# A hybrid layer on one core: norm_g held in PSUM, the Newton step in scalar form, one instruction for the key low parts, tile 5's counts on DVE, and a schedule from other durations

## The chip, the core and the metric

The kernel runs on one core of one Trainium2 chip. The core has a matrix engine (TensorE, PE in the profile; its weight loads are PEld), three engines for the element-wise work (VectorE or DVE, ScalarE or ACT, GpSimd or POOL) and SyncE (SP), which here issues every DMA. They share SBUF (128 partitions) and PSUM (8 banks of 128 x 2 KB), in which PE puts its products. The metric is the time of one execution on the device in microseconds (us); lower is better.

## What is computed

One layer with 1024 tokens of 1024 channels, in float32. The input projection of the normed x feeds a pooling mixer (A), an attention over keys that an indexer picks (B, "dsa") and an attention with forget gates (C, "fox"); each is gated, and an output projection, the residual and a last norm follow. Cut to what matters:

```python
h = rmsnorm(x, norm_g)                       # y * rsqrt(mean(x*x) + 1e-6) * g
(pv, pg, dq, dk, dv, dg, iq, ik, iw, fq, fk, fv, fg, ff) = split_columns(h @ w_in)
a_out = pool_mixer(pv, pool_w, pool_scale) * silu(pg)   # windows 2, 4, 8, 16
# B: the indexer scores every key, 8 heads of 32 channels, and keeps the 256 best a query
score = sum_h(iw[h] * relu(iq[h] . ik))      # only keys of the query's 64-chunk or before
b_out = softmax_attention(dq, dk, dv, keys=top_k(score, 256)) * silu(dg)
# C: F = cumsum(log_sigmoid(ff + fox_bf)); causal
c_out = softmax_attention(fq, fk, fv, bias=F[t] - F[s]) * silu(fg)
out = rmsnorm(x + concat(a_out, b_out, c_out) @ w_out, final_g)
```

## The kernel before

**Order.** The kernel doesn't run in the order in which it is written. Each instruction is given to `Plan.op` with its engine, what it reads and writes, a duration and a priority; `schedule` then goes through all of them once, on a model clock, and always takes the instruction that can start first on its engine (of those that can start together, the one of lowest priority number). The durations come from `t_act`, `t_dve`, `t_pool` and `t_mm`, by the number of columns (a negative number marks a transpose on PE). The result is one fixed list per engine, and a buffer for every result: SBUF and PSUM are cut into tags, each with a few slots, which are handed out in the same walk. Priorities put the norms first (`PR_NORM` 0), then the indexer's scores (`PR_DOT` 1), weights (1.5), the attention (`PR_AT` 2), the search (`PR_SEL` 5) and the projections (`PR_PJ` 10); the evictions of projections, `PR_EV`, have -10. The projections are so the work that PE does while it has nothing more urgent.

**Numbers in two parts.** For most products a float32 value is split into a high part in the fast format and a low part, the difference. A product is then three (high x high, high x low, low x high), all through line L462. So behind most transposes and weight loads stand two instructions: ScalarE copies the high part, DVE or POOL subtracts the low part.

**Stages.** Tiles are 128 tokens.

1. Norms and indexer projection, for tiles 0 to 7. `norm`: ScalarE sums the squares; `rstd` makes mean + eps (L481, L484) on DVE, the power -0.5 on POOL (L486) and one Newton step on DVE in three instructions of one column (L487, L489, L490); DVE multiplies x by that and by norm_g (L515, two halves); PE transposes (L522); ScalarE copies the high part (L526) and DVE subtracts the low part (L527). The norm weights are brought to 128 partitions by two PE products with ones, which ScalarE copies to SBUF (L418). `idx_proj` makes 302 columns a tile (L462): ScalarE copies 288 of them (L544), DVE takes the six of the forget gate (L545) and the eight head weights (L547). `idx_k` repeats the key four times (POOL, `rep`, L553), transposes it (L563), and has ScalarE copy it (L565) and DVE turn the rows 32 to 63 and 96 to 127 into low parts (L567, two instructions of 32 partitions).
2. Scores, `idx_tile`, for tiles 2 to 7: PE products per head (L595), ScalarE's relu (L599), DVE's multiply and add (L603, L607).
3. Search for the 256th best score of each query, `search`: 31 iterations over the bits of the threshold. In each one the scores of the tiles 2 to 7 are counted against the present threshold, those of `on_act` (5, 6, 7) by ScalarE (L771, 768 to 1024 columns), those of 2, 3, 4 by DVE (L776, 384 to 640 columns); then DVE decides in three instructions of six columns (L790, L792, L793). `finish` (L805 to L849) makes the masks on DVE; for the tiles of `on_act` it has a few more instructions. PE does the projections in this stretch: fox k and q, values, gates, and the pooling mixer's input.
4. `gate`: ScalarE's tanh into a buffer of tag `th` (L736), DVE's multiply with the product (L738), which ends the use of the PSUM bank; then it is stored. The tag `th` has two buffers. `pool_tile` uses the same tag: window sums on POOL, DVE's L1073, a product by PE (L1081), DVE's multiply with the stored gate in a `th` buffer (L1085) and the store of that to `mix`.
5. Attention, six units each of fox and dsa: products (L919, L922), DVE with bias or mask (L930), exponential (L941), transposes (L956), high and low parts (L963, L965), products with the values (L969, L974).
6. Output projection, eight tiles.

All DMAs go through SP's one queue (L365), also in the list's order. PSUM banks are shared by tags: `pj` (projections) has three, `s` (scores; also the key transposes and the pool products) has 2 and 3, `pn` (transposes of the norm) has 4, 5 and 7. PE begins with 60 products on the identity matrix that nothing reads (L408).

## Time and profile before

| what | value |
|---|---|
| time, median of 3 runs | 649.95 us (649.72 to 651.6) |
| the profiled execution's own time | 651.98 us |
| its span (first to last instruction) | 650.2 us |
| PE busy in it | 627.8 us, 97% |
| DVE, ACT, POOL busy | 474.4, 425.5, 201.6 us |

The span is what the profile's rows lie in, and all positions are counted from its start. "Busy" of PE counts a product as long as it is in the engine at the rate it has, not at its best. In the table of stretches the granted clock is given as a share: 1.00 is the 2.4 GHz level, 0.50 the 1.2 GHz one. A timeline names what an instruction waited for in brackets, the idle time of its engine ahead of it and the instruction that ended it.

### The profile page before, as it was taken

What the parts mean: (1) busy time and instruction counts of PE and PEld (TensorE: products, weight loads), DVE (VectorE), ACT (ScalarE), POOL (GpSimd) and SP (SyncE); (2) the same over time, 40 slices, a digit from 0 to 9 for tenths busy, and PEclk for the clock granted to TensorE, in tenths of its full rate; (3) what the DMA queues carried; (4) which work ended last, traced back from release to release, by engine and by line L of the source; (5) the groups of instructions that cost most, each with busy time, mean ns of one, the idle gap of its engine ahead of it and who ended that gap; (6) DMA issues with size and microseconds to landing.
All of it is one profiled execution on the core that took longest, in us unless ns stands there. A gap on an engine that the chain in (4) does not pass through costs nothing. (4 is left out here: it accounts for less than half of the span.)

```text
span 650.2 us, 10279 instructions
## 1 busy us (share of the span) xinstructions
PE 627.8 (97%) x3280; PEld 529.0 (81%) x3280; DVE 474.4 (73%) x1187; ACT 425.5 (65%) x945; POOL 201.6 (31%) x218
## 2 busy tenths in 40 slices
PE   8799999999999999799999999999999999999995
PEld 7698777789988999588888888888888687788884
DVE  5987999877776887889997768766757877643322
ACT  6645678698899888513478776688477879622121
POOL 3510212450017640126252614312131625232211
PEclk9999999999999999989999999999999999999999
DMA  8616453461026337845669678599946554547311
GB/s 241 192 53 176 148 156 109 129 184 44 0 87 157 103 127 208 196 124 138 176 200 247 202 211 212 155 252 270 242 162 169 166 165 148 157 161 226 120 43 66
DMA packets 95380, 102.72 MB, mean 158 GB/s; under 512 B 8055, under 2 KB 64471, under 8 KB 95326
## 3 DMA queue, kind: packets, MB, share of 16 engines
q1 hardware_dynamic: 95326, 102.07, 55.3%
q8 instruction: 26, 0.43, 0.3%
q14 instruction: 28, 0.23, 0.1%
HBM read 72.09 MB, written 29.96 MB: 157 GB/s over the span
## 5 line engine op out<-in xcount | busy, mean ns | idle before, releaser
L462 PE MATMUL bank<-RA 128*128 128x512 f32 (+2 forms) x2016 | 481.4, 378 | 3.8 <-DVE FA L738 3.8
L462 PEld LDWEIGHTS bank<-RA 128*128 128x128 f32 x2016 | 359.7, 189 | 54.0 <-DVE FA L738 4.3
L771 ACT ACTIVATE FA<-FA 128x768 bf16<-128x768 f32 (+2 forms) x96 | 99.6, 1037 | 15.8 <-DVE FA L793 12.4
L695 POOL TENSOR_TENSOR RA<-FA,RA 128x512 fp32r<-128x512 f32 x44 | 60.2, 1382 | 145.7 <-ACT RA L694 129.4
L941 ACT ACTIVATE FA<-FA 128x512 f32<-128x512 f32 (+3 forms) x144 | 86.8, 605 | 19.2 <-DVE FA L936 19.0
L963 ACT ACTIVATE RA<-bank 128x512 fp32r<-128x512 f32 (+1 forms) x120 | 64.5, 552 | 41.5 <-PE bank L956 36.7
L930 DVE CUSTOM_DVE_ANT_0 FA<-bank,FA 128x512 f32<-128x512 f32 (+3 forms) x144 | 77.3, 550 | 19.6 <-PE bank L922 11.2
L965 DVE TENSOR_TENSOR RA<-bank,RA 128x512 fp32r<-128x512 f32 (+1 forms) x120 | 74.1, 634 | 20.2 <-ACT RA L963 18.5
L956 PE MATMUL bank<-FA 128*128 128x128 f32 x432 | 72.6, 275 | 1.0 <-ACT FA L941 1.0
L776 DVE TENSOR_SCALAR_CACHE_REDUCE FA<-FA 128x384 bf16<-128x384 f32 (+2 forms) x96 | 71.2, 742 | 1.9
L956 PEld LDWEIGHTS bank<-FA 128*128 128x128 f32 x432 | 53.6, 140 | 20.9 <-ACT FA L941 4.3
L607 DVE SCALAR_TENSOR_TENSOR FA<-FA 128x512 f32<-128x512 f32 (+3 forms) x70 | 52.8, 776 | 2.3
L919 PE MATMUL bank<-RA 128*128 128x512 f32 (+3 forms) x144 | 52.1, 362 | 0.3 <-DVE FA L930 0.2
L974 PE MATMUL bank<-RA 128*128 128x512 f32 (+3 forms) x144 | 50.1, 376 | 0.5 <-DVE RA L965 0.5
L922 PE MATMUL bank<-RA 128*128 128x512 f32 (+3 forms) x144 | 50.1, 352 | 0.0
L599 ACT ACTIVATE FA<-bank 128x512 f32<-128x512 f32 (+3 forms) x80 | 39.7, 527 | 15.1 <-PE bank L595 6.2
L926 POOL TENSOR_TENSOR FA<-FA 128x128 f32<-128x128 f32 x48 | 29.1, 610 | 65.4 <-DVE FA L930 45.5
L969 PE MATMUL bank<-RA 128*128 128x512 f32 (+3 forms) x144 | 45.4, 341 | 0.3 <-DVE FA L1003 0.3
L1123 POOL TENSOR_TENSOR RA<-FA,RA 128x1024 fp32r<-128x1024 f32 x8 | 19.2, 2399 | 46.4 <-ACT RA L1122 35.3
L1135 DVE TENSOR_TENSOR FA<-bank,FA 128x512 f32<-128x512 f32 x16 | 11.0, 687 | 30.9 <-PE bank L462 30.9
L1007 POOL TENSOR_TENSOR FA<-FA 128x512 f32<-128x512 f32 x12 | 16.1, 1348 | 56.0 <-DVE FA L1003 35.9
L919 PEld LDWEIGHTS bank<-RA 128*128 128x128 f32 x144 | 27.1, 188 | 6.2 <-DVE FA L930 2.5
(145 smaller groups left out, 689.1 us busy)
## 6 DMA issues: line engine op xcount, KB each, us to landing
FA<-in_w_in_dram SPq DMA_DIRECT2D x60, 256.0 KB, 3.8
FA<-in_x_dram SPq DMA_DIRECT2D x15, 512.0 KB, 4.1
RA<-qk_fq SPq DMA_DIRECT2D x12, 512.0 KB, 8.2
RA<-qk_dq SPq DMA_DIRECT2D x12, 512.0 KB, 11.2
RA<-qk_dk SPq DMA_DIRECT2D x18, 256.0 KB, 6.0
...
```

Source lines behind the costliest of these rows:

```text
L462: M(lambda: nc.tensor.matmul(p()[:, :n], fa(), fb(), start=st, stop=sp), n, keys, [p], pr)
L607: V(lambda rl=rl, w=w, acc=acc, wc=wc: nc.vector.scalar_tensor_tensor(acc(), rl()[:, :w], wc(), acc(), op0=OP.mult, op1=OP.add), w, [rl, ( ...
L695: G(lambda raw=raw, s=s: nc.gpsimd.tensor_tensor(Wl()[:, s, :], raw(), f32(Wh()[:, s, :]), op=OP.subtract), 512, [raw, (Wh, kh)], [(Wl, kh ...
L771: A(lambda c=c, i=i, jk=jk, s=s: nc.scalar.activation(jk(), SC[i](), AF.Sign, bias=s(), scale=-1.0, accum_out=cn()[:, c:c + 1]), n, sck(i) ...
L776: V(lambda c=c, i=i, jk=jk, s=s: nc.vector.tensor_scalar(jk(), SC[i](), s(), None, op0=OP.is_lt, op1=OP.add, accum_out=cn()[:, c:c + 1]), ...
L919: M(lambda s=s, k=k, n=n, j=j, hd=hd: nc.tensor.matmul(s()[:, :n], q()[:, hd, j * 128:j * 128 + 128], k()[:, hd, :n], start=True, stop=False),
L922: M(lambda s=s, k=k, n=n, j=j, hd=hd: nc.tensor.matmul(s()[:, :n], q()[:, 2 + hd, j * 128:j * 128 + 128], k()[:, hd, :n], start=False, sto ...
L930: V(lambda s=s, Pt=Pt, n=n, u=u, j=j, mx=mx, bias=bias: nc.vector.tensor_tensor_reduce(Pt()[:, :n], s()[:, :n], bias()[:, u * 512:u * 512 ...
L941: A(lambda Pt=Ps[j][u], n=n, j=j, u=u, hd=hd, nm=nm: nc.scalar.activation(Pt()[:, :n], Pt()[:, :n], AF.Exp, bias=nm()[:, j:j + 1], accum_o ...
L956: M(lambda pt=pt, j=j, d=d, Pt=Ps[j][kb // 4], c=kb % 4 * 128: nc.tensor.transpose(pt()[:, j * 128 - d:j * 128 - d + 128], Pt()[:, c:c + 1 ...
L963: A(lambda ph=ph, pt=pt, c=c: nc.scalar.activation(ph()[:, c], pt()[:, c], AF.Copy), n, [pt], [ph], pr, psum=True)
L965: V(lambda ph=ph, pl=pl, pt=pt, c=c: nc.vector.tensor_tensor(pl()[:, c], pt()[:, c], f32(ph()[:, c]), op=OP.subtract), n, [pt, ph], [pl], pr)
```

## The change

In the programs' text, ahead of the plan:

- `norm_g` stays in PSUM. The two products with ones go to a new tag `gb` in the banks 2 and 3 (those of tag `s`), ScalarE's two copies L418 are gone, and DVE's norm multiply reads its factor from there. The key transposes move from tag `s` to `pn`.
- The Newton step, before (v * r0) * r0, then times -0.5 plus 1.5, then times r0, is written as three `tensor_scalar` with the power r0 as a scalar operand. The first, v * -0.5, doesn't need r0. It stands in the output norms too.
- The two L567 become one instruction on 128 partitions, with a column of 0 and -1 that tells which rows become low parts.
- L545 and L547 go to POOL and read ScalarE's copy, which now takes all the columns to 302, at a priority 0.5 later.
- Tile 5's counts go from ScalarE to DVE: per iteration DVE counts four tiles, ScalarE two.

And what the plan believes:

- A lock: an instruction of DVE with two inputs in SBUF (`two`) or of a fast form (`fast`), and one of POOL over 4 columns, can't run at the same time in the plan.
- Durations: ScalarE with a sum 0.1 us longer, a search count another 0.02; PE products 0.01 us longer, transposes 0.0025 shorter; POOL's repeat of the key shorter, pool sums at 800 and the copy at 412 units for 1024 and 1600.

```diff
+                    if o.lock:
+                        t = max(t, port)
...
+            if o.lock:
+                port = t + o.dur
...
-    return (0.052 if psum else 0.094) + n / 1200.0 + (0.093 if acc else 0.0)
+    return (0.052 if psum else 0.094) + n / 1200.0 + (0.193 if acc else 0.0)
...
-    return 0.07 if n < 0 else max(n * 0.41667e-3 + 0.003, 0.107)
+    return 0.0675 if n < 0 else max(n * 0.41667e-3 + 0.0135, 0.107)
...
+    P.tag("gb", "PS", 1, [2, 3])
...
-    V = lambda fn, n, r, w, pr=0.0, two=False, acc=False, fast=1: P.op(DVE, fn, t_dve(n, two, acc, fast), r, w, pr)
-    G = lambda fn, n, r, w, pr=0.0: P.op(POOL, fn, t_pool(n), r, w, pr)
+    V = lambda fn, n, r, w, pr=0.0, two=False, acc=False, fast=1: P.op(DVE, fn, t_dve(n, two, acc, fast), r, w, pr,
+                                                                       lock=two or fast > 1)
+    G = lambda fn, n, r, w, pr=0.0: P.op(POOL, fn, t_pool(n), r, w, pr, lock=n > 4)
...
-    gb = P.new("gb", [128, D])
+    gb = [P.new("gb", [128, 512]) for _ in range(2)]
...
-        A(lambda pb=pb, u=u: nc.scalar.activation(gb()[:, u * 512:u * 512 + 512], pb(), AF.Copy), 512, [pb], [(gb, u)],
-          -99, psum=True)
...
-        V(lambda: nc.vector.scalar_tensor_tensor(a(), r0(), r0(), v(), op0=OP.mult, op1=OP.mult), 1,
-          [(b, 0), (b, 1)], [(b, 2)], pr, two=True)
-        V(lambda: nc.vector.tensor_scalar(a(), a(), -0.5, 1.5, op0=OP.mult, op1=OP.add), 1, [(b, 2)], [(b, 2)], pr)
-        V(lambda: nc.vector.tensor_tensor(r(), r0(), a(), op=OP.mult), 1, [(b, 1), (b, 2)], [(b, 3)], pr)
+        V(lambda: nc.vector.tensor_scalar(a(), v(), -0.5, None, op0=OP.mult), 1, [(b, 0)], [(b, 2)], pr)
+        V(lambda: nc.vector.tensor_scalar(a(), a(), r0(), r0(), op0=OP.mult, op1=OP.mult), 1, [(b, 1), (b, 2)],
+          [(b, 2)], pr)
+        V(lambda: nc.vector.tensor_scalar(r(), a(), 1.5, r0(), op0=OP.add, op1=OP.mult), 1, [(b, 1), (b, 2)],
+          [(b, 3)], pr)
...
+            V(lambda c=c, u=u: nc.vector.scalar_tensor_tensor(xt()[:, c], xt()[:, c], r(), gb[u](), op0=OP.mult,
+                                                              op1=OP.mult), 512, [kx[u], kr, gb[u]], [kx[u]], pr)
...
-        V(lambda: nc.vector.tensor_tensor(FFA()[:, i * NH:i * NH + NH], p()[:, 296:302], bfb(), op=OP.add), 6,
-          [p, k_bfb], [(cc, "ff", i)], pr)
...
+        G(lambda: nc.gpsimd.tensor_tensor(FFA()[:, i * NH:i * NH + NH], z()[:, 296 - zo:302 - zo], bfb(), op=OP.add), 6,
+          [z, k_bfb], [(cc, "ff", i)], pr + 0.5)
...
-        pk = P.new("s", [128, 512])
+        pk = P.new("pn", [128, 512])
...
-        for r in (32, 96):
-            V(lambda r=r: nc.vector.tensor_tensor(kk()[r:r + 32], pk()[r:r + 32, :128], f32(kk()[r:r + 32]),
-                                                  op=OP.subtract), 128, [pk, (KI, i)], [(KI, i)], pr)
+        V(lambda: nc.vector.scalar_tensor_tensor(kk(), f32(kk()), lom(), pk()[:, :128], op0=OP.mult, op1=OP.add), 128,
+          [pk, (KI, i), k_lom], [(KI, i)], pr)
...
-                                              op=OP.add), 1024, ksrc, [(dst, "d")], pr)
+                                              op=OP.add), 800, ksrc, [(dst, "d")], pr)
...
-            G(lambda: nc.gpsimd.tensor_copy(s2()[0:64, 16:], s1()[0:64, 16:]), 1600, [(s1, "d")], [(s2, "d")], pr)
+            G(lambda: nc.gpsimd.tensor_copy(s2()[0:64, 16:], s1()[0:64, 16:]), 412, [(s1, "d")], [(s2, "d")], pr)
...
-    on_act = [5, 6, 7]
-    tiles = on_act + [2, 3, 4]
+    on_act = [6, 7]
+    tiles = on_act + [2, 3, 4, 5]
```

Lines of the new program are a few numbers higher: L481 is L487, L515 is L522, L527 is L533, L738 is L743, L776 is L781, L790 to L793 are L795 to L798, L805 is L810, L819 is L824, L841 is L846, L1081 and L1085 are L1086 and L1090, SP's L365 is L370. The new Newton step is L493, L494 and L496; the new key low part is L572.

How the order of each engine moves shows best at three places. First DVE in the norms, some 40 instructions from its start (names: RA and FA are SBUF, FA the plain float32 part; bank_ is a PSUM bank). Before:

```order
L527 TENSOR_TENSOR RA<-bank_72,RA 128x4x128
L487 SCALAR_TENSOR_TENSOR FA<-FA 128x1
L489 TENSOR_SCALAR FA<-FA 128x1
L490 TENSOR_TENSOR FA<-FA 128x1
L487 SCALAR_TENSOR_TENSOR FA<-FA 128x1
L515 SCALAR_TENSOR_TENSOR FA<-FA 128x512 x2
L545 TENSOR_TENSOR FA<-bank_71,FA 128x6
L547 TENSOR_SCALAR FA<-bank_71 128x8
```

The same place after the change:

```order
L572 SCALAR_TENSOR_TENSOR RA<-RA,FA,bank_70 128x128
L493 TENSOR_SCALAR FA<-FA 128x1
L533 TENSOR_TENSOR RA<-bank_72,RA 128x4x128
L494 TENSOR_SCALAR FA<-FA 128x1
L496 TENSOR_SCALAR FA<-FA 128x1
L487 TENSOR_SCALAR FA<-FA 128x1
L522 SCALAR_TENSOR_TENSOR FA<-FA,bank_67 128x512
L533 TENSOR_TENSOR RA<-bank_69,RA 128x4x128
L522 SCALAR_TENSOR_TENSOR FA<-FA,bank_68 128x512
```

The Newton step now is three instructions of the form of the old L489, the first of them apart from the others; the small evictions of the projection are gone from between; the norm multiply reads a bank.

Second, DVE at the end of the search. Before, from behind the last decision and one pool multiply (L1085) on:

```order
L807 TENSOR_SCALAR FA<-FA 128x3
L808 TENSOR_TENSOR FA<-FA 128x3
L819 TENSOR_SCALAR FA<-FA 128x384
L841 TENSOR_SCALAR FA<-FA 128x384
L838 TENSOR_SCALAR FA<-FA 128x1
L819 TENSOR_SCALAR FA<-FA 128x512
L843 SCALAR_TENSOR_TENSOR FA<-FA 128x384
L838 TENSOR_SCALAR FA<-FA 128x1
L841 TENSOR_SCALAR FA<-FA 128x512
L845 SCALAR_TENSOR_TENSOR FA<-FA 128x384
L843 SCALAR_TENSOR_TENSOR FA<-FA 128x512
L847 SCALAR_TENSOR_TENSOR FA<-FA 128x384
```

The next instruction there is the first L738, the gate's multiply, which ends the use of a projection's bank. After the change, from the last decision on:

```order
L798 SCALAR_TENSOR_TENSOR FA<-FA 128x6
L810 TENSOR_SCALAR FA<-FA 128x2
L812 TENSOR_SCALAR FA<-FA 128x2
L813 TENSOR_TENSOR FA<-FA 128x2
L824 TENSOR_SCALAR FA<-FA 128x384
L743 SCALAR_TENSOR_TENSOR FA<-FA,bank_66 128x512
L843 TENSOR_SCALAR FA<-FA 128x1
L824 TENSOR_SCALAR FA<-FA 128x512
```

The gate's multiply (L743) stands behind one mask pass; both pool multiplies of the second pool tile (L1090) stand 12 and 14 rows ahead of L810, in the last but one iteration, and none stands behind the search.

Third, SP's queue at the same time: loads of fox k and q for the first attention units, stores of values (vd), the pool results (mix) and the last gates. Before:

```order
L365 DMA RA<-qk_fk_90 64x2x512 x2
L365 DMA RA<-qk_fq_92 64x4x512
L365 DMA vd_81<-RA 128x768
L365 DMA RA<-qk_fq_92 64x4x512
L365 DMA RA<-qk_fk_91 64x2x512 x2
L365 DMA RA<-qk_fk_94 64x2x512 x2
L365 DMA RA<-qk_fq_93 64x4x512 x2
L365 DMA FA<-in_w_in_dram 128x4x128 x2
L365 DMA mix_82<-FA 128x512
L365 DMA mix_83<-FA 128x512
```

After the change:

```order
L370 DMA RA<-qk_fk_90 64x2x512 x2
L370 DMA RA<-qk_fq_92 64x4x512
L370 DMA vd_81<-RA 128x768
L370 DMA RA<-qk_fq_92 64x4x512
L370 DMA RA<-qk_fk_91 64x2x512 x2
L370 DMA RA<-qk_fk_94 64x2x512 x2
L370 DMA mix_82<-FA 128x512
L370 DMA RA<-qk_fq_93 64x4x512
L370 DMA mix_83<-FA 128x512
L370 DMA RA<-qk_fq_93 64x4x512
```

The two stores of the second pool tile move ahead of a load each of the last q and of the weights.

## Rows read from the trace of the kernel before

**Rows 1.** Page, part 1: busy us of each engine, instructions.

```profile
PE 627.8 (97%) x3280; PEld 529.0 (81%) x3280; DVE 474.4 (73%) x1187; ACT 425.5 (65%) x945; POOL 201.6 (31%) x218
```

**Rows 2.** Table of stretches: length; PE, PEld, DVE, ACT, POOL; clock; DMA.

```profile
12.50:36.00 23.50, 19.03 (x147) 18.01 (x145) 21.29 (x54) 14.95 (x33) 11.31 (x15) 1.00 0.65 195
60.00:110.00 50.00, 47.69 (x219) 38.01 (x218) 47.73 (x86) 37.05 (x80) 11.00 (x14) 1.00 0.49 149
110.00:264.00 154.00, 154.00 (x765) 137.41 (x764) 120.78 (x322) 134.32 (x253) 49.12 (x38) 1.00 0.42 119
252.60:271.40 18.80, 18.19 (x77) 14.04 (x76) 14.25 (x47) 14.46 (x27) 2.54 (x2) 1.00 1.06 247
275.20:282.00 6.80, 6.01 (x14) 4.77 (x15) 6.80 (x14) 1.23 (x2) 0.14 (x1) 0.50 0.20 77
300.00:570.00 270.00, 267.91 (x1487) 220.75 (x1486) 201.71 (x528) 193.14 (x489) 89.49 (x91) 1.00 0.71 194
```

**Rows 3.** Timeline of PE, 262 to 277: start, duration, instructions, [wait ahead].

```profile
268.14 1.12 PE L1081 MATMUL bank<-FA 128*128 128x512 f32 x2 [0.61 <-DVE FA L1085]
...
270.62 1.55 PE L462 MATMUL bank<-RA 128*128 128x512 f32 x6
275.99 1.22 PE L462 MATMUL bank<-RA 128*128 128x512 f32 x2 [3.82 <-DVE FA L738]
```

**Rows 4.** Timeline of PE, 15 to 36, its four waits.

```profile
18.42 0.66 PE L522 MATMUL bank<-FA 128*128 128x128 f32 x4 [0.80 <-DVE FA L515]
20.19 0.66 PE L522 MATMUL bank<-FA 128*128 128x128 f32 x4 [1.12 <-DVE RA L527]
...
28.23 0.33 PE L563 MATMUL bank<-FA 128*128 128x128 f32 x1 [1.33 <-POOL FA L553]
...
31.65 0.66 PE L522 MATMUL bank<-FA 128*128 128x128 f32 x4 [1.22 <-DVE RA L527]
```

**Rows 5.** Timeline of DVE, 22 to 28, two instructions of the Newton steps.

```profile
22.95 1.31 DVE L490 TENSOR_TENSOR FA<-FA 128x1 f32<-128x1 f32 x1
24.18 1.33 DVE L487 SCALAR_TENSOR_TENSOR FA<-FA 128x1 f32<-128x1 f32 x1
```

**Rows 6.** Timeline of POOL, 21 to 31.

```profile
22.95 2.54 POOL L695 TENSOR_TENSOR RA<-FA,RA 128x512 fp32r<-128x512 f32 x2
```

**Rows 7.** Groups by line and shape, whole span: busy us, mean ns | idle before.

```profile
L515 DVE SCALAR_TENSOR_TENSOR FA<-FA 128x512 f32<-128x512 f32 x16 | 11.6, 752 | 0.2
L738 DVE SCALAR_TENSOR_TENSOR FA<-FA,bank 128x512 f32<-128x512 f32 x16 | 10.9, 682 | 6.6 <-ACT FA L736 6.5
...
L487 DVE SCALAR_TENSOR_TENSOR FA<-FA 128x1 f32<-128x1 f32 x16 | 6.6, 415 | 10.5 <-POOL FA L486 10.5
L490 DVE TENSOR_TENSOR FA<-FA 128x1 f32<-128x1 f32 x16 | 5.7, 356 | 0.5
...
L567 DVE TENSOR_TENSOR RA<-bank,RA 32x128 fp32r<-32x128 f32 x16 | 4.6, 290 | 3.3 <-ACT RA L565 2.9
...
L489 DVE TENSOR_SCALAR FA<-FA 128x1 f32<-128x1 f32 x16 | 2.4, 152 | 0.5
...
L819 DVE TENSOR_SCALAR_CACHE_REDUCE FA<-FA 128x768 bf16<-128x768 f32 x2 | 2.0, 1009 | 0.0
```

**Rows 8.** One line's instructions: ns min/median/max, first and last start.

```profile
L790 DVE TENSOR_SCALAR FA<-FA x31: 165/170/1377, 128.8 to 264.8; 128x6 int32<-128x6 int32 x31
```

**Rows 9.** Timeline of ACT, 266 to 279.

```profile
273.56 1.23 ACT L736 ACTIVATE FA<-bank 128x512 f32<-128x512 f32 x2 [5.29 <-DMA mix<-FA]
```

**Rows 10.** Timeline of SP's queue, 249 to 278.

```profile
251.10 1.29 SPq L365 DMA_DIRECT2D RA<-qk_fk  x2
...
268.11 2.31 SPq L365 DMA_DIRECT2D mix<-FA  x2
```

**Rows 11.** One line's instructions: ns min/median/max, first and last start.

```profile
L793 DVE SCALAR_TENSOR_TENSOR FA<-FA x31: 160/167/172, 133.3 to 268.5; 128x6 int32<-128x6 int32 x31
```

**Rows 12.** Timeline of DVE, 268 to 277, the first mask pass.

```profile
270.25 0.61 DVE L819 TENSOR_SCALAR_CACHE_REDUCE FA<-FA 128x384 bf16<-128x384 f32 x1
```

More of the change, by code (lines that the diff above doesn't have):

```diff
@@ L77 @@
 class Op:
-    __slots__ = ("eng", "fn", "dur", "pr", "seq", "deps", "bufs", "outs", "end", "left", "bytes", "lag", "tr")
+    __slots__ = ("eng", "fn", "dur", "pr", "seq", "deps", "bufs", "outs", "end", "left", "bytes", "lag", "tr", "lock")
 class Plan:
@@ L109, in new, with op @@
         return b
[L111 removed]
+    def op(self, eng, fn, dur, r=(), w=(), pr=0.0, nbytes=0, lag=0.0, tr=False, lock=False):
         o = Op()
         o.eng, o.fn, o.dur, o.pr, o.seq, o.bytes, o.lag = eng, fn, dur, pr, self.seq, nbytes, lag
[L114 removed]
+        o.tr, o.lock = tr, lock
         self.seq += 1
@@ L172, in schedule @@
         n = len(self.ops)
-        was_tr = False
+        was_tr, port = False, 0.0
         while len(order) < n:
@@ L397, in tile_trunk @@
     bfb, k_bfb = carve(NH)
+    lom, k_lom = carve(1)
+    for r, c in ((0, 0.0), (32, -1.0), (64, 0.0), (96, -1.0)):
+        G(lambda r=r, c=c: nc.gpsimd.memset(lom()[r:r + 32], c), 1, [], [k_lom])
     xt0 = P.new("xt", [128, D])
@@ L414, in tile_trunk @@
     for u in range(2):
-        pb = P.new("pj", [128, 512])
-        P.op(PE, lambda pb=pb, u=u: nc.tensor.matmul(pb(), grow()[:, D:], grow()[:, u * 512:u * 512 + 512], start=True,
-                                                     stop=True), 1.7, [(grow, 0), (grow, 1)], [pb], -99)
-        A(lambda pb=pb, u=u: nc.scalar.activation(gb()[:, u * 512:u * 512 + 512], pb(), AF.Copy), 512, [pb], [(gb, u)],
-          -99, psum=True)
+        P.op(PE, lambda u=u: nc.tensor.matmul(gb[u](), grow()[:, D:], grow()[:, u * 512:u * 512 + 512], start=True,
+                                              stop=True), 1.7, [(grow, 0), (grow, 1)], [gb[u]], -99)
     ld(bfb, lambda: bass.AP(tensor=fox_bf.tensor, offset=fox_bf.offset, ap=[[0, 128], [1, NH]]), 3000, w=[k_bfb],
@@ L485, in rstd @@
               k_ss[1:] + [(b, 0)], [(b, 0)], pr, two=True)
-        P.op(POOL, lambda: nc.gpsimd.tensor_tensor(r0(), v(), half(), op=OP.pow), 0.47, [(b, 0), k_half], [(b, 1)], pr)
-        V(lambda: nc.vector.scalar_tensor_tensor(a(), r0(), r0(), v(), op0=OP.mult, op1=OP.mult), 1,
-          [(b, 0), (b, 1)], [(b, 2)], pr, two=True)
-        V(lambda: nc.vector.tensor_scalar(a(), a(), -0.5, 1.5, op0=OP.mult, op1=OP.add), 1, [(b, 2)], [(b, 2)], pr)
-        V(lambda: nc.vector.tensor_tensor(r(), r0(), a(), op=OP.mult), 1, [(b, 1), (b, 2)], [(b, 3)], pr)
+        P.op(POOL, lambda: nc.gpsimd.tensor_tensor(r0(), v(), half(), op=OP.pow), 0.5, [(b, 0), k_half], [(b, 1)], pr)
+        V(lambda: nc.vector.tensor_scalar(a(), v(), -0.5, None, op0=OP.mult), 1, [(b, 0)], [(b, 2)], pr)
[3 more added lines that the diff above has]
+          [(b, 3)], pr)
         return r, (b, 3)
@@ L514, in norm @@
             c = slice(u * 512, u * 512 + 512)
-            V(lambda c=c: nc.vector.scalar_tensor_tensor(xt()[:, c], xt()[:, c], r(), gb()[:, c], op0=OP.mult,
-                                                         op1=OP.mult), 512, [kx[u], kr, (gb, u)], [kx[u]], pr,
-              two=True)
+            V(lambda c=c, u=u: nc.vector.scalar_tensor_tensor(xt()[:, c], xt()[:, c], r(), gb[u](), op0=OP.mult,
+                                                              op1=OP.mult), 512, [kx[u], kr, gb[u]], [kx[u]], pr)
         for u in range(2):
@@ L541, in idx_proj @@
         zo = 0 if i > 1 else 256
-        z = P.new("z", [128, 288]) if i > 1 else P.new("zs", [128, 32])
+        z = P.new("z", [128, 302]) if i > 1 else P.new("zs", [128, 46])
         Z[i] = z
-        A(lambda: nc.scalar.activation(z(), p()[:, zo:288], AF.Copy), 288 - zo, [p], [z], pr, psum=True)
-        V(lambda: nc.vector.tensor_tensor(FFA()[:, i * NH:i * NH + NH], p()[:, 296:302], bfb(), op=OP.add), 6,
-          [p, k_bfb], [(cc, "ff", i)], pr)
-        V(lambda: nc.vector.tensor_scalar(iwb()[:, 8 * i:8 * i + 8], p()[:, 288:296], 8.0 ** -0.5, None, op0=OP.mult),
-          8, [p], [(cc, "iw", i)], pr)
+        A(lambda: nc.scalar.activation(z(), p()[:, zo:302], AF.Copy), 302 - zo, [p], [z], pr, psum=True)
+        G(lambda: nc.gpsimd.tensor_tensor(FFA()[:, i * NH:i * NH + NH], z()[:, 296 - zo:302 - zo], bfb(), op=OP.add), 6,
+          [z, k_bfb], [(cc, "ff", i)], pr + 0.5)
+        G(lambda: nc.gpsimd.tensor_scalar(iwb()[:, 8 * i:8 * i + 8], z()[:, 288 - zo:296 - zo], 8.0 ** -0.5, None,
+                                          op0=OP.mult), 8, [z], [(cc, "iw", i)], pr + 0.5)
     def rep(i, h0, n, pr):
@@ L933, in unit @@
                       [s] + ([(nf, b) for b in range(4 * u, min(4 * u + 4, t + 1))] if fox else [(maskb, t)]),
-                      [Pt, (mx, j, u)], pr, two=True)
+                      [Pt, (mx, j, u)], pr)
             km = [(mx, j, u) for j in range(4) for u in range(g + 1)]
```

12 lines of the change are left out of this document (5 added, 7 removed).

## The prediction

> **What bounds the kernel now.** I read the busy times first: TensorE (PE) has work in 627.8 of the 650.2 us [rows 1], and the order has the same 3336 PE instructions before and after. The time can only change by what PE waits, by the clock it is granted, and by what lies ahead of its first product and behind its last. Next, the table of stretches [rows 2]: it is there to show where PE is not full. From 110 to 264 us it is full to the hundredth, from 300 to 570 it lacks 2.1 us in 270. It lacks 4.5 us in 12.5 to 36 (norms and indexer projection), 2.3 us in 60 to 110 (indexer scores), and around 272 comes the one long hole, 3.82 us, after which the granted clock is 0.50 (the 1.2 GHz level) from 275.2 to 282.0 [rows 2, 3]. These three places hold the whole gain that is to be had; last, I read who releases PE at each.
>
> **Place 1, the norms (12.5 to 36 us).** PE waits there 0.80, 1.12, 1.33 and 1.22 us [rows 4], 4.47 in all, for DVE's norm multiply (L515), for its low parts (L527) and, at 28.23, for a POOL copy. The copy is late because of DVE: L490 and L487, on one column each, take 1.31 and 1.33 us [rows 5], and the second ends with the two POOL subtractions L695 that ran from 22.95 to 25.49 [rows 6]. They are blocked by POOL, not slow: over the run L489 has a mean of 152 ns, L487 415 and L490 356 [rows 7]. Behind them in DVE's queue stand L515 and L545/L547, and ScalarE's L544 and the copy come after those.
>
> What the change takes off DVE per tile: the three Newton steps cost 0.415 + 0.152 + 0.356 = 0.92 us, and become three tensor_scalar, the form of L489, 3 x 0.152 = 0.46; the first of them needs no result of POOL, so two lie behind the power. Saved 0.46. The two L515 read norm_g from PSUM, as L738 reads its bank: 0.682 for 0.752, saved 0.14. Two L567 become one of the same 128 columns: saved 0.29 (between 0, if the wider instruction costs both, and 0.29). L545 and L547 go to POOL: two short ones like L489, 0.30 [rows 7]. Together 1.2 us a tile, some 10 us over eight tiles, while DVE is busy 21.3 of the 23.5 us from 12.5 to 36 [rows 2]. On POOL 16 small instructions come in; at the mean of what it ran there, 11.3 us for 15 [rows 2], 12 us at most, some 1.5 a tile. POOL has them behind the copy that PE waits for, and their readers are the scores and the forget gates, so I cost them nothing. If POOL were late with them, the first score multiply would wait.
>
> Banks 2 and 3 now hold norm_g until the last L515, and the key transposes share three other banks. In the order, the first score product stands after the same PE work as before to within 1 us, so I cost this at nothing; if the norms fell behind, the scores would wait. Of the 4.47 us I take 3.3, because the loads of x and of weights and ScalarE's order (square of the next tile ahead of L526) stay. Bounds: 0.8, if only the wait through the copy goes for the most part, and 4.5. The two copies of norm_g leave ScalarE ahead of the second half square, but PE runs warm-up products in order until then, 51 instead of 52 ahead of the first projection: 0.1. Together **3.4**.
>
> One rule speaks against this step. L489 is never blocked at one column, but the same kind of instruction is, at six: L790 takes 165 ns at the least and 1377 at the most [rows 8]. The Trainium skill (SBUF — State Buffer, "Who interferes with whom") says that tensor_scalar can enter modes that take the port pair shared with GpSimd. By that rule the new Newton steps would be held as the old ones were, and it is a rival below; the row of L489 speaks for one column being exempt.
>
> **Place 2, the scores (60 to 110 us).** PE lacks 2.3 us, waiting for score banks behind ScalarE, and DVE is busy 47.7 of 50 [rows 2]. Nothing here gets cheaper. The plan now knows that a DVE instruction with two SBUF inputs and a POOL one exclude each other, and the order spreads the score products wider: the last has 2 us more PE work ahead of it. I take **1.5**, between -1 (a worse mix) and 2.3.
>
> **Place 3, the end of the search (264 to 282 us).** The chain: PE stops at 270.62 + 1.55 = 272.17 for a bank [rows 3]. The bank is freed by DVE's L738, which starts late for two reasons. ScalarE's tanh L736 waits 5.29 us until 273.56 [rows 9] for its buffer, which still held the pool mixer's result; its store was issued at 268.11, behind the loads of fox q and k [rows 10]. And in DVE's order the finish (thresholds and mask passes) stands between the search's end and L738. PE loses 3.82 us here and 6.8 us at half clock, worth 3.4; 0.61 more is a wait for the second pool product [rows 3]. Sum 7.8.
>
> What the change makes of it: the plan's cheaper pool chain brings both pool products of tile 1 ahead by some 8 us of PE work, both L1085 stand more than one iteration ahead of the search's end (one stood after it), and the two stores are ahead of each half of the last q load. At about 4.5 us an iteration, L1085 and its store come some 7 us earlier, near 262. The loads and one store that stand ahead of it in the queue from 251.1 on [rows 10] are about 2.9 MB by their shapes in the order, and at the 247 GB/s of that stretch [rows 2] they take 12 us, to 263: the store lands between 263 and, with queues beside it, 267, ahead of the last count. So the tanh no longer waits, and DVE decides: after L793 come three short instructions of 0.17 like it [rows 11], one mask pass of 0.61 and L738 with 0.68 [rows 7, 12], some 1.9 us. The search ended at 268.5 + 0.2 [rows 11]; 268.7 + 1.9 = 270.6, ahead of the 272.2 at which PE needs the bank, by 1.6 us.
>
> That holds if the search keeps step, and **tile 5's counts** decide it. An iteration takes (268.5 - 133.3) / 30 = 4.51 us [rows 11]. DVE is busy 120.8 of 154 us, 78% [rows 2], 3.53 us an iteration. The 32 added counts have a like in L819 on the same 768 columns, 1.009 us [rows 7]; the next instruction starts a little before its end, so 0.95 to 1.01. The new iteration needs 4.48 to 4.54 us of DVE: the search becomes DVE's instead of ScalarE's, at nearly the same length, -1 to +1 us over 31 iterations, with no slack. Both PE and the scores arrive earlier by places 1 and 2, DVE perhaps less than PE. Against the 1.6 us of margin I leave PE a wait of 1.5 us, and no fall of the clock, since the waits of 0.8 to 1.33 us of place 1 were in a stretch at 1.00 [rows 2, 4]. Gain **6.3**, between 1 (a 3.4 us wait and the clock falls again) and 7.8.
>
> **The rest.** The attention reads the same data in another mix of products; PE lacks 2.1 us there and the order has 171 returns from transposes to products for 175: 0, between -4 and 2. The outputs' Newton steps lie behind PE's products except in the last tile, one short instruction less: **0.2**. Sum 3.4 + 1.5 + 6.3 + 0.2 = 11.4. It is made against the profiled execution, 651.98 us (1.8 outside its span), which is 2.0 above the median of three; the difference is taken off the median, 649.95 - 11.4 = **638.5 us**.
>
> **Rivals.**
> 1. The search falls behind: 0.1 us more an iteration is 3.1 us, L738 is 1.5 to 3 us late, the clock falls again, place 3 gains about 0.5: 649.95 - 5.6 = 644.3. For it: DVE at 100% has no slack, and POOL holds L790 for up to 1.4 us [rows 8]. Against: that loss is in the 3.53 already.
> 2. The Newton steps are blocked: place 1 gives 1.4, 640.5.
> 3. The new order does not do on the chip what the plan says: the stages that were full get holes. One wait like that of place 1 (about 1 us) in most of the attention's twelve units costs 10 us, 648.5. For it: DVE and ScalarE orders are changed everywhere, and a stage that is full can only lose. Against: PE lacks so little there now that the old plan, with the cruder durations, already fits.
> 4. Slower: the search overruns by 0.5 us an iteration, because ScalarE's and DVE's evictions queue behind four counts in a row. 15.5 us late, less the margin of 1.6, is a wait of 14, and with 3.4 of clock 17.4 for the 7.8 of now: 649.95 - 5.1 + 9.6 = 654.5. It turns slower than before once the wait is over 9.5 us, from 0.36 us an iteration. For it: 78% and 21% fill DVE. Against: an eviction blocks counts for 0.68 us only and is in the 78%.
>
> **How the numbers follow.** Forecast 0.62; rival 1 0.14; rival 2 0.06; rival 3 0.11; rival 4 0.07. About 0.3% (2 us) is what a measurement of this kernel can tell from no change: faster means under 648.0. Forecast and rivals 1 and 2 are faster, and a third of rival 3: 0.86; within 0.3%: 0.07 of rival 3's rest; slower: rival 4, 0.07. All terms at their upper ends give 17.6, near 632.5; the upper end takes in rival 1, 645.5. Rivals 3 and 4 stay out, 0.18.
>
> **What would show it.** Place 1: L493, L494 and L496 of the new kernel near 150 ns each with none over 0.3, and waits of PE from 12.5 to 36 that add up to about 1.2. Place 3: no PE wait over 2 us, no stretch at 0.50 between 250 and 300, tanh not waiting for a mix store. The search: 30 intervals of L798 at 4.4 to 4.6 us, DVE over 95% busy in them. It would be wrong if PE's holes moved into 300 to 570, or if an iteration came out over 4.6.

## The result, and the profile after

The changed kernel takes 658.94 us (median; 658.18 to 659.48), the kernel before 649.84 beside it: 1.0138 times as long, 95% interval 1.0111 to 1.0165. 638.5 was forecast, in a range from 632.5 to 645.5. The profiled execution after took 658.52 us with a span of 656.6, against 651.98 and 650.2: the rows below show 6.5 of the 9.1 us between the medians.

PE is busy 626.8 us, 1.0 less than before [rows 1], but lacks 29.8 us of its span where it lacked 22.4. The table of stretches of the changed kernel (columns as in [rows 2]; the rows answer to its first three and its last, with two stretches of low clock between) says where:

```profile
12.50:36.00 23.50, 23.13 (x175) 21.99 (x174) 20.86 (x54) 16.96 (x37) 12.55 (x27) 1.00 0.74 217
60.00:110.00 50.00, 48.91 (x224) 38.53 (x223) 47.02 (x82) 35.14 (x75) 11.24 (x15) 1.00 0.47 138
110.00:264.00 154.00, 147.31 (x722) 131.16 (x721) 146.23 (x363) 97.98 (x179) 47.63 (x36) 0.99 0.36 104
220.00:228.00 8.00, 6.00 (x24) 5.68 (x24) 7.79 (x18) 4.63 (x11) 4.56 (x5) 0.79 0.20 46
304.00:312.00 8.00, 6.52 (x21) 5.29 (x22) 7.96 (x17) 0.63 (x1) 2.19 (x2) 0.60 0.41 131
300.00:570.00 270.00, 261.96 (x1447) 217.39 (x1448) 198.30 (x525) 188.44 (x480) 88.22 (x95) 0.99 0.70 193
```

The norms lack 0.37 us where they lacked 4.47, the scores 1.09 where they lacked 2.31: 5.3 won. From 110 to 264 us, where PE was full, it now lacks 6.69, with DVE busy 95% for 78% and ScalarE 64% for 87%; from 300 to 570 it lacks 8.04 where it lacked 2.09. PE's timeline names the waits (columns as in [rows 3], which answer to them; L468 are projections, L924 the first attention products):

```profile
221.01 6.00 PE L468 MATMUL bank<-RA 128*128 128x384 f32 x24 [2.62 <-ACT FA L1055]
229.30 3.08 PE L468 MATMUL bank<-RA 128*128 128x384 f32 x16 [2.29 <-DVE RA L670]
...
245.60 13.93 PE L468 MATMUL bank<-RA 128*128 128x384 f32 x71 [1.79 <-DVE RA L670]
...
267.69 0.47 PE L924 MATMUL bank<-RA 128*128 128x512 f32 x1 [3.01 <-DMA RA<-qk_fq]
...
277.62 22.07 PE L468 MATMUL bank<-RA 128*128 128x512 f32 x96 [1.13 <-DVE FA L743]
305.48 0.58 PE L924 MATMUL bank<-RA 128*128 128x256 f32 x1 [5.78 <-DVE FA L935]
```

16.6 us, against 4.6 between 200 and 310 before (4.43 of it in [rows 3]), and the clock falls twice, around the waits of 2.62 and 5.78, to means of 0.79 and 0.60 over 8 us.

The first three have one cause. The line of the search's last decision (ns min/median/max, first and last start; below it the page's sum of who waited for it, us and times) has (274.6 - 129.3) / 30 = 4.84 us an iteration for 4.51 [rows 11], and ScalarE's counts (L776) wait 53.8 us for it, where before they (L771) waited 12.4, as the last row, of the kernel before, says:

```profile
L798 DVE SCALAR_TENSOR_TENSOR FA<-FA x31: 156/166/1233, 129.3 to 274.6; 128x6 int32<-128x6 int32 x31
...
  ACT FA L776: 53.8, 29
...
  ACT FA L771: 12.4, 20
```

DVE's and then POOL's timeline at 207 us show what makes a decision late. Three instructions on six columns, 0.17 us each when free, end where POOL's instructions end (206.37 + 1.89 = 208.26, 208.22 + 1.30 = 209.52, 209.60 + 1.89 = 211.49):

```profile
207.07 1.22 DVE L797 TENSOR_TENSOR FA<-FA 128x6 int32<-128x6 f32 x1
208.32 1.23 DVE L798 SCALAR_TENSOR_TENSOR FA<-FA 128x6 int32<-128x6 int32 x1
...
210.12 1.40 DVE L795 TENSOR_SCALAR FA<-FA 128x6 int32<-128x6 int32 x1
```

```profile
206.37 1.89 POOL L1062 TENSOR_TENSOR FA<-FA 128x1024 f32<-128x1024 f32 x1 [0.31 <-ACT FA L1055]
208.22 1.30 POOL L445 TENSOR_TENSOR RA<-FA,RA 128x512 fp32r<-128x512 f32 x1
209.60 1.89 POOL L1062 TENSOR_TENSOR FA<-FA 64x1024 f32<-64x1024 f32 x1
```

Two more instructions of DVE in the search, on sixteen columns, belong to the pool mixer. They take 170 and 175 ns in the mean before, and here, for the first pool tile, DVE's timeline has

```profile
221.68 1.20 DVE L1080 TENSOR_TENSOR FA<-FA 128x16 f32<-128x16 f32 x1
...
223.67 1.28 DVE L1082 TENSOR_TENSOR FA<-FA 128x16 f32<-128x16 f32 x1
```

They too end where POOL's do (222.85 and 224.92), and the decision L798 at 226.24 comes 7.16 us after the one before it. And ScalarE's timeline at 219 us shows how that reaches PE, though ScalarE is idle a third of the time: the eviction L1055 that PE waits for stands in ScalarE's order behind a count, and the count waits 1.49 us for the decision:

```profile
219.34 1.04 ACT L776 ACTIVATE FA<-FA 128x896 bf16<-128x896 f32 x1 [1.49 <-DVE FA L798]
...
220.38 0.57 ACT L1055 ACTIVATE FA<-bank 128x512 f32<-128x512 f32 x1
...
226.50 1.04 ACT L776 ACTIVATE FA<-FA 128x896 bf16<-128x896 f32 x1 [3.37 <-DVE FA L798]
...
227.54 0.47 ACT L669 ACTIVATE RA<-bank 128x384 fp32r<-128x384 f32 x1
```

The other waits follow from the same late search, as the queues' order says. The load of fox q, for which PE waits 3.01 us, stands in SP's queue behind stores of values that wait for the evictions L670; the loads of fox k and q begin at 257.10, for 251.10 before [rows 10]:

```profile
249.81 7.24 SPq L370 DMA_DIRECT2D vd<-RA  x3
257.10 1.29 SPq L370 DMA_DIRECT2D RA<-qk_fk  x2
```

At 305 the attention's first bias instructions (L935) wait in DVE's order behind the mask passes, which begin with the search's end.

### The profile page after: what moved, and what is told of

It reads as the page before. It is cut to its first block, busy times and chain, and to the rows that moved or that the text cites. A ratio compares the mean times of both kernels' runs of the same rounds, so it can differ in the third digit from the quotient of the medians.

```text
span 656.6 us, 10254 instructions
## 1 busy us (share of the span) xinstructions
PE 626.8 (95%) x3280; PEld 529.0 (81%) x3280; DVE 501.9 (76%) x1219; ACT 394.8 (60%) x879; POOL 197.1 (30%) x238
## 5 line engine op out<-in xcount | busy, mean ns | idle before, releaser
L468 PE MATMUL bank<-RA 128*128 128x512 f32 (+2 forms) x2016 | 478.3, 378 | 7.8 <-DVE RA L670 4.1
L468 PEld LDWEIGHTS bank<-RA 128*128 128x128 f32 x2016 | 361.5, 190 | 59.2 <-DVE RA L670 4.7
L781 DVE TENSOR_SCALAR_CACHE_REDUCE FA<-FA 128x384 bf16<-128x384 f32 (+3 forms) x128 | 103.5, 809 | 2.6
L776 ACT ACTIVATE FA<-FA 128x896 bf16<-128x896 f32 x64 | 69.8, 1091 | 57.0 <-DVE FA L798 53.8
L700 POOL TENSOR_TENSOR RA<-FA,RA 128x512 fp32r<-128x512 f32 x44 | 58.7, 1346 | 144.5 <-ACT RA L699 140.0
L935 DVE CUSTOM_DVE_ANT_0 FA<-bank,FA 128x512 f32<-128x512 f32 (+3 forms) x144 | 76.8, 551 | 25.5 <-PE bank L927 13.6
L946 ACT ACTIVATE FA<-FA 128x512 f32<-128x512 f32 (+3 forms) x144 | 86.8, 606 | 12.6 <-DVE FA L941 12.4
L961 PE MATMUL bank<-FA 128*128 128x128 f32 x432 | 71.1, 274 | 1.6 <-DVE RA L970 1.5
L924 PE MATMUL bank<-RA 128*128 128x512 f32 (+3 forms) x144 | 52.1, 362 | 9.7 <-DVE FA L935 6.5
L612 DVE SCALAR_TENSOR_TENSOR FA<-FA 128x512 f32<-128x512 f32 (+3 forms) x70 | 51.1, 749 | 2.0 <-DVE FA L612 0.2
L931 POOL TENSOR_TENSOR FA<-FA 128x128 f32<-128x128 f32 x48 | 23.4, 490 | 79.7 <-DVE FA L935 48.9
L924 PEld LDWEIGHTS bank<-RA 128*128 128x128 f32 x144 | 27.2, 189 | 17.9 <-DVE FA L935 11.4
L699 ACT ACTIVATE RA<-FA 128x512 fp32r<-128x512 f32 x44 | 26.7, 627 | 12.4 <-PE bank L468 12.4
```

Source lines behind the costliest of these rows:

```text
L468: M(lambda: nc.tensor.matmul(p()[:, :n], fa(), fb(), start=st, stop=sp), n, keys, [p], pr)
L612: V(lambda rl=rl, w=w, acc=acc, wc=wc: nc.vector.scalar_tensor_tensor(acc(), rl()[:, :w], wc(), acc(), op0=OP.mult, op1=OP.add), w, [rl, ( ...
L700: G(lambda raw=raw, s=s: nc.gpsimd.tensor_tensor(Wl()[:, s, :], raw(), f32(Wh()[:, s, :]), op=OP.subtract), 512, [raw, (Wh, kh)], [(Wl, kh ...
L776: P.op(ACT, lambda c=c, i=i, jk=jk, s=s: nc.scalar.activation(jk(), SC[i](), AF.Sign, bias=s(), scale=-1.0, accum_out=cn()[:, c:c + 1]), t ...
L781: V(lambda c=c, i=i, jk=jk, s=s: nc.vector.tensor_scalar(jk(), SC[i](), s(), None, op0=OP.is_lt, op1=OP.add, accum_out=cn()[:, c:c + 1]), ...
L924: M(lambda s=s, k=k, n=n, j=j, hd=hd: nc.tensor.matmul(s()[:, :n], q()[:, hd, j * 128:j * 128 + 128], k()[:, hd, :n], start=True, stop=False),
```

## The experiments

All ratios are against the kernel before on the same chip. Theory 1 is the one above. Theory 2 is that the new order makes the holes, whoever counts; the later ones came up on the way, and the expectations say what each is.

**The change taken apart.** Tile 5 back on ScalarE, all else as changed:

```diff
-    on_act = [6, 7]
+    on_act = [5, 6, 7]
```

> The changed kernel with tile 5's counts back on ScalarE, all else as changed. Theory 1 (the counts take DVE's last slack, POOL's work then stretches the search, evictions and masks come late and PE waits 2.78, 2.45, 1.96, 3.17, 1.29 and 5.95 us between 218 and 305): these waits go, an iteration comes back to 4.5 us, and 640 to 647 us come out. Theory 2 (the new order from other durations and the lock makes the holes, whoever counts): most of the waits stay, 652 to 660 us.

Run e1: 659.75 us, 1.0144 (1.0113 to 1.0174). Theory 1 was right on the place and wrong on the time: PE waits for nothing from 110 to 300 us (154.00 busy of 154.00 and 36.00 of 36.00), yet the total is no better. The time has moved to the last attention units: 85.31 us busy of the 100 from 440 to 540. The largest wait there, in PE's timeline:

```profile
492.43 0.80 PE L974 MATMUL bank<-RA 128*128 128x512 f32 x1 [7.00 <-DVE FA L1008]
```

The other way round, the kernel before with nothing but tile 5 on DVE (`on_act = [6, 7]`):

> The kernel before with only tile 5's counts on DVE. Theory 1: slower, 657 to 663 us, iterations near 4.85 us, new waits of PE in 200 to 300. Theory 2: within 2 us of before, 648 to 652, since the old order is kept.

Run e2: 654.95 us, 1.0068 (1.0047 to 1.0088): slower, with 4.85 us an iteration, but only waits of 0.62 and 0.76 us inside the search; 4.21 for fox q at 266 and 2.89 for L738 at 282 make the rest. The sign is theory 1's, the size between the two.

The plan alone, and the norms' edits alone. The plan's part has lock, durations and POOL's costs, and one thing more that the list of the change leaves out: the attention's bias instruction (L930, now L935) is planned without `two`, so 0.06 us shorter and free of the lock. No run takes that back by itself.

> The kernel before with only the plan changed: lock, durations, POOL costs. Theory 1: 645 to 650 us; the pool products and their stores come earlier and part of the 3.82 us wait before 276 goes. Theory 2: 653 to 660 us, with waits of several us in 200 to 305 that before does not have.

Run e3: 655.56 us, 1.0075 (1.0048 to 1.0101; single runs from 651.0 to 659.4). Theory 2 was right on the time, on the waits less so: the search takes 4.96 us an iteration with no wait of PE from 200 to 300 us, and 2.12 us for L935 at 302 is the first; from 300 to 570 PE lacks 12.0 us of 270.

> The kernel before with only the edits in the norms: norm_g in PSUM, scalar Newton step, one key low part instruction, two evictions on POOL. Both theories: PE's waits from 12.5 to 36 us fall from 4.5 to about 0.5 us, and 644 to 647 us come out, if the rest of the order stays as it was.

Run e4: 655.35 us, 1.0071 (1.0049 to 1.0093). A miss for both theories, and the lesson on a gain ahead of a full stage. Its profiled run (652.1, the faster end of its 652.0 to 656.8) has won nearly all of the norms' waits: 0.38 and 0.33 us are left of 4.47. PE then comes earlier to the first attention product, and stands there:

```profile
259.28 0.77 PE L919 MATMUL bank<-RA 128*128 128x512 f32 x1 [3.29 <-DMA RA<-qk_fq]
...
274.98 15.25 PE L463 MATMUL bank<-RA 128*128 128x512 f32 x59 [3.11 <-DVE FA L738]
```

PE is ready for that product at 259.28 - 3.29 = 255.99, where before it reached it at 263.06 without a wait; the loads of k and q ahead of it begin at 249.50, where they began at 251.10 [rows 10]. PE is 7 us earlier, its load 1.6. The second wait is the one of 3.82 us before: ScalarE's tanh again waits for a mix store. The clock falls once more than before, too.

**One suspected cost taken out, the order kept row for row.** First 0.65 us of DVE an iteration, by a shorter count of tile 5:

```diff
-  tensor_scalar(jk(), SC[i](), s(), None, op0=OP.is_lt, ...)
+  tensor_scalar(jk()[:, :e], SC[i]()[:, :e], s(), None, op0=OP.is_lt, ...)   # e = 128 for tile 5
```

> The changed kernel with its order kept row for row, but tile 5's count reads 128 of its 768 columns (and compares with 64.5), so its mask is not the reference's; 0.65 us less DVE in each of 31 iterations. Theory 1 (DVE without slack in the search): an iteration falls from 4.84 to 4.2 to 4.4 us, PE's waits at 218, 227, 244, 276 and 299 us go, with them the two falls of the clock, and 641 to 647 us come out. Theory 2 (the order makes the holes): iterations shorten, but 654 us or more.

Run e5: 645.86 us, 0.9929 (0.9909 to 0.9949): 13 us off the changed kernel, as theory 1 said. (264.1 - 130.1) / 30 = 4.47 us an iteration, a little over its range. Of the waits of the list above 1.77 us at 225, 0.81 for fox q and 3.91 for L935 are left. Two falls of the clock stay, against what it said, from 225.8 and from 294.1 on. Then POOL's part, its subtractions cut to an eighth in that stretch:

> The changed kernel with its order kept, but POOL's subtractions of the weights that are used from the pool gates to the fox gates work on an eighth of their columns (the products take the high part in place of the low one there, so those projections are less exact than the reference's). Theory 1, as I now hold it (POOL's subtractions stop DVE's decision instructions, ScalarE's next count waits for the decision, and evictions stand behind that count): the decision instructions of over 0.5 us become rare outside the pool sums, an iteration takes 4.2 to 4.5 us, 644 to 651 us. Rival (DVE's own work is too much, POOL has no part): iterations stay at 4.75 us or more, 656 us or more.

Run e6: 646.25 us, 0.9925 (0.9896 to 0.9954), 4.53 us an iteration, at the rim of theory 1's range. The waits at 221, 229 and 246 are gone; 3.09 us at 260 and 4.04 for L935's like at 295 are left. The count of tile 5 is the full one here, so DVE's own work is not too much by itself: it is too much with POOL's holds. The three decision instructions together take 0.98 us an iteration in the changed kernel, 0.67 here (means 218, 219 and 230 ns), 0.50 if never held. The means of the changed kernel:

```profile
L797 DVE TENSOR_TENSOR FA<-FA 128x6 int32<-128x6 f32 x31 | 11.3, 365 | 2.7
...
L798 DVE SCALAR_TENSOR_TENSOR FA<-FA 128x6 int32<-128x6 int32 x31 | 10.5, 337 | 1.0
...
L795 DVE TENSOR_SCALAR FA<-FA 128x6 int32<-128x6 int32 x31 | 8.6, 278 | 0.0
```

**Is it the plan's view of the DMAs?** Two runs with loads planned slower:

```diff
-                dma_free[0] = st + o.bytes / 270e3
+                dma_free[0] = st + o.bytes / 225e3
```

> Tile 5 on ScalarE as in the run with 659.8 us, and the plan counts a DMA at 225 GB/s in place of 270. Theory 3 (its 23 us of waits from 450 to 535 come from loads that the chip does slower than the plan believes, with ScalarE's copies of the output weights and evictions queued behind them): those waits shrink to under 8 us, 640 to 649 us. Theory 4 (the waits come from the order of products alone): 655 us or more.

> The norms' edits alone, and the plan counts a DMA at 225 GB/s. Theory 3 (the gain of the norms is given back at a wait of 3.45 us for the first fox q, which lands later than planned): that wait falls under 1 us, 645 to 650 us. Theory 4: 653 us or more.

Runs e7 and e8: 667.48 us (1.0251, 1.022 to 1.0281) and 669.18 (1.0282, 1.0258 to 1.0307): theory 3 falls. The first still waits 4.13 us for a load of dsa q at 489 and 9.34 for L1008 at 508, the second 3.31 and 6.26 at 267 and 279. What makes them this much worse than e1 and e4 was not followed up.

**A lighter search.** Tile 2, the smallest, to ScalarE beside 6 and 7:

```diff
-    on_act = [6, 7]
-    tiles = on_act + [2, 3, 4, 5]
+    on_act = [2, 6, 7]
+    tiles = on_act + [3, 4, 5]
```

> The changed kernel with tile 2's counts (384 columns) on ScalarE beside 6 and 7, so that DVE counts 3, 4 and 5: 0.7 us less DVE an iteration than the change, ScalarE 0.6 us more. Theory 1 (DVE without slack under POOL): an iteration of 4.4 to 4.6 us, the waits of PE from 218 to 277 us gone, 641 to 647 us. Theory 5 (what counts is how well the plan's iteration fits the chip's, not DVE's load): the plan again doesn't know that POOL stops the decision, so waits of 2 to 3 us in 200 to 300 stay, 651 us or more.

Run e9: 644.96 us, 0.9908 (0.9875 to 0.9942), (265.6 - 129.9) / 30 = 4.52 us an iteration: faster than both kernels, with the reference's whole computation. Its rows for the stretch and for the decision:

```profile
110.00:264.00 154.00, 153.53 (x760) 136.71 (x759) 134.32 (x329) 127.15 (x254) 49.86 (x38) 1.00 0.44 124
```

```profile
L798 DVE SCALAR_TENSOR_TENSOR FA<-FA x31: 157/166/2292, 129.9 to 265.6; 128x6 int32<-128x6 int32 x31
...
  ACT FA L776: 10.5, 12
```

ScalarE waits 10.5 us for decisions where it waited 53.8, and PE lacks 0.5 us of 154. POOL's holds are still there (L795 takes up to 2.82 us, L798 up to 2.29); DVE again has a wait for ScalarE's counts, 14.0 us in all ahead of L797, which can cover the holds of L795 ahead of it. The same with tiles 3, 5 and 7 on ScalarE (its result is not the reference's: DVE's count of tile 6 writes 896 columns into a scratch buffer of 768; the work is the same):

> The changed kernel with tiles 3, 5 and 7 on ScalarE and 2, 4 and 6 on DVE: 0.65 us less DVE an iteration than the change, ScalarE about 0.7 us more. Theory 1: 4.4 to 4.7 us an iteration, 641 to 649 us. Theory 5: 651 us or more, with waits of 2 to 3 us in 200 to 300.

Run e12: 643.41 us, 0.9883 (0.9858 to 0.9908). Theory 1 again.

**Does the plan have to know?** The lock does not hold for the decision's instructions, nor for the pool mixer's two. Here it does (the cut shows one of the five), first with tile 5, then with tile 2:

```diff
-     ... op0=OP.bitwise_xor), nq, [kc], [kn], pr)
+     ... op0=OP.bitwise_xor), nq, [kc], [kn], pr, two=True)
```

> The changed kernel with one thing more in the plan: the three decision instructions and the two 16-column ones of the pool mixer also exclude POOL's. Tile 5 stays on DVE, the computation is the same. Theory 5: PE's waits in 200 to 260 us go, since evictions are planned where they can run; as the search is no shorter (4.8 us an iteration), the projections that PE does meanwhile are missing as filling later, and waits of 1 to 2 us come near 480 to 530 us; 650 to 658 us. Theory 1: waits of over 1.9 us at two or more places in 200 to 260 us stay, 657 us or more.

> Both: tile 2's counts on ScalarE, and the plan knows that POOL stops the decision. Theory 1: 641 to 648 us as without the plan's knowledge. Theory 5: waits in 200 to 300 us under 2 us in all, some in 480 to 530, 648 to 656 us.

Runs e10 and e11: 662.74 us (1.0172, 1.0149 to 1.0196) and 658.71 (1.0118, 1.0096 to 1.0139). The waits went about where theory 5 put them: with tile 5, 1.01 and 2.31 us are left in 200 to 260 for 2.62, 2.29 and 1.79, and PE lacks 8.9 of the 40 us from 500 to 540. With tile 2, PE is full from 110 to 300, as in the first run, and lacks 6.7 us from 500 to 540. Both totals are worse than theory 5 said, and theory 1's 641 to 648 for the second is missed by 11: a lighter search is not enough. What is missing there is projections to fill in. The table of stretches for their line alone, 500 to 540 us, for the kernel before, the change, the first run (tile 5 on ScalarE), e9 and e10 in turn (PE's busy time and count, clock, DMA):

```profile
500.00:540.00 40.00, 17.55 (x51) 1.00 0.51 146
```

```profile
500.00:540.00 40.00, 17.02 (x53) 1.00 0.88 223
```

```profile
500.00:540.00 40.00, 1.11 (x3) 0.87 0.60 154
```

```profile
500.00:540.00 40.00, 15.65 (x52) 1.00 0.67 185
```

```profile
500.00:540.00 40.00, 1.31 (x4) 0.96 0.76 206
```

A search that keeps PE full or nearly so (154.00 and 150.67 us of the 154 from 110 to 264) but ends late (275.3 and 278.0 us for the third and fifth, 265.6 for e9) has spent the projections that would cover the last attention units. A late search is not the only way to spend them: in e8 it ends at 262.0, and only 10 of these products are left.

**Why the first run's search is long.** 4.88 us an iteration, with the split that before does in 4.51. Either the longer ScalarE durations in the plan do it, or the lock. (A search count is planned another 0.12 us longer than other sums, not the 0.02 of the list of the change.)

> The changed kernel with tile 5's counts on ScalarE (as in the run with 659.8 us) and ScalarE's two longer durations taken back to the old ones in the plan (0.1 us a sum, 0.12 us a count); lock and the rest as changed. Theory 6 (the plan that believes in longer counts puts evictions and copies ahead of them, so the search, whose end decides how many projections are left to fill the last attention units, takes 4.9 us an iteration): 4.4 to 4.6 us an iteration, over 40 projection products left for 500 to 540 us, no wait of over 2 us there, 640 to 648 us. Theory 7 (the lock makes the search long): 4.8 us an iteration, 655 us or more.

> The changed kernel with tile 5's counts on ScalarE, with the longer durations but no lock in the plan. Theory 6: the search stays at 4.8 to 5.0 us an iteration, under 20 projection products are left for 500 to 540 us, 652 us or more. Theory 7: 4.5 us an iteration, 640 to 648 us.

Runs e13 and e14: 654.09 us (1.004, 1.0022 to 1.0059) and 655.77 (1.0079, 1.0049 to 1.011). It is the durations: with the old ones 4.56 us an iteration and 56 projection products left for 500 to 540; without the lock 4.86 and 25. But theory 6 missed the first time by 6 us: with the shorter search the waits in front of evictions came back, 0.5 to 0.9 us four times from 219 to 245, 4.19 at 263 and 3.07 at 293.

> Tile 2's counts on ScalarE beside 6 and 7, and ScalarE's old durations in the plan. Theory 6: a shorter search than in the run with 645.0 us, below 4.5 us an iteration, and 638 to 645 us. Theory 7: as that run, 645 us.

> The kernel before with the norms' edits and tile 2 in place of tile 5 on ScalarE; the plan as before. Theory 6: the old plan with a balanced search has iterations of 4.2 to 4.5 us; the waits for fox q near 255 and for the gate's multiply near 271 us may stay, 643 to 651 us. If the lock and new durations were what helps the run with 645.0 us: 653 us or more.

Runs e15 and e16: 654.25 us (1.0056, 1.0036 to 1.0077) and 658.04 (1.0105, 1.0084 to 1.0126). The first has the shortest search of all the full ones, (256.3 - 125.2) / 30 = 4.37 us, and is slower than e9: 2.31, 1.27 and 0.94 us of waits for L670 in the search and 4.44 for fox q. The second shows that the gain of tile 2 needs the new plan's order.

What stays open is what an order must have to suit the chip. Two ways of losing are shown, evictions behind late counts and projections spent early; that e9 avoids both at once was found by trial, and e15 against e9 says that neither a short search nor a light DVE is enough.

## Why the prediction was wrong

- **Place 1, the norms**: right. 3.4 forecast, the stretch gives 4.1. The sizes inside were off: L493, L494 and L496 take 154, 272 and 214 ns (0.64 for 0.46), L522 743 ns for 682; the new key low part takes 343 ns where two took 580. The likes were badly chosen. L489 and L738 have constants as their scalars, while L496 reads one scalar operand from SBUF, L494 two and L522 one, and each comes with some 60 ns more (154, 214, 272; 678 against 743). Against L515, which has the same operand, reading norm_g from PSUM saves 9 ns, so nothing. The rival of blocked Newton steps did not come about, but the run is a weak test of it: none of the sixteen L494 and only one L496 began while POOL had over 0.3 us of an instruction to go (that L496 took 206 ns). Six L493 did, and none took over 156. The Trainium skill (SBUF — State Buffer, "Who interferes with whom") says that a tensor_scalar can contend with GpSimd when its operands meet certain conditions. The trace agrees for the six-column L795, up to 1403 ns, and shows no hold of one column; the prediction's rule had no conditions.
- **Place 2, the scores**: right, 1.2 for 1.5.
- **Place 3**: the end of the search went as written in part. There is no wait for a mix store, and one mask pass stands ahead of L743. PE's wait of 1.13 us there for the 1.5 that I left is luck: the bank comes at 277.6 instead of 270.6, and PE, held up by its own waits, is there at 276.5 instead of 272.2. Not as written is a wait of 3.01 us for fox q, so that PE lacks 4.44 us from 264 to 300 as it lacked 4.43 before; of the 6.3 us only the fall of the clock is won there, 3.4.
- **The step that failed** is the sentence "The new iteration needs 4.48 to 4.54 us of DVE", and "at nearly the same length". It came out at 4.84. I had added the counts to DVE's busy time of before, with POOL's holds of before in it and no idle time. The table of stretches over the 30 iterations, before and after, and for e6:

```profile
133.30:268.50 135.20, 134.59 (x678) 121.48 (x677) 104.67 (x301) 120.95 (x227) 40.96 (x31) 1.00 0.43 121
```

```profile
129.30:274.60 145.30, 135.60 (x671) 121.41 (x670) 139.19 (x362) 90.38 (x164) 37.12 (x29) 0.99 0.38 108
```

```profile
130.30:266.20 135.90, 132.81 (x668) 119.41 (x667) 129.79 (x363) 91.06 (x165) 19.61 (x29) 1.00 0.40 113
```

DVE is busy 139.19 / 30 = 4.64 us an iteration, and idle 0.20, in some four gaps of 0.03 to 0.1 us between its instructions; before it was busy 3.49 and idle 1.02. The holds grew: those of the three decision instructions are 0.48 us an iteration (0.98 less 0.50) for 0.35 before (0.85 less 0.50). So of the 0.33 us over the middle of my range 0.13 are holds and 0.20 idle time that the sum left out. With holds of 0.17 the third row has 4.33 busy and the same 0.20 idle. And there is no cover any more. Before, DVE waited for ScalarE's counts ahead of L792, 22.6 us in all, and a hold of L790, which stands ahead of that wait, could lie under it:

```profile
L792 DVE TENSOR_TENSOR FA<-FA 128x6 int32<-128x6 f32 x31 | 7.9, 255 | 22.8 <-ACT FA L771 22.6
```

- **What I priced at nothing** was the search's inside. I let a late search cost time only at its end, at L738. ScalarE's evictions stand behind its counts, so each late decision can stop PE in the middle: 6.69 us lacking from 110 to 264, and one fall of the clock, 1.7 us more. This and the next point are the largest losses.
- **The rest at 0, between -4 and 2**: the stretch from 300 on lost 5.95, below the range, most of it in one wait of 5.78 for L935 that begins 0.3 us ahead of it, since the masks begin when the search ends. e9 still has 2.96 there, before 0.17.
- **The rivals**: the fourth named the mechanism (evictions behind counts) and gave it 0.07, with one wait at the end as its price; it came at 0.33 us an iteration, short of the 0.36 from which I let it be slower, because it costs in several places. The third (holes in full stages) is not what made this result, as e5 and e6 show with the order kept, but it is what the same plan does with tile 5 on ScalarE.
- **The sum** added gains of places as if each were kept. e4 shows that the gain of the norms, put alone into the old kernel, is given back at a load and a store that don't come earlier. Its upper end is added up wrongly, too: the upper ends of the terms give 16.9 us (4.5 + 0.1 + 2.3 + 7.8 + 2 + 0.2), not 17.6, and so 633.1.
